# A hybrid encoder block: the inverse second stage of the long convolutions in three float32r part products, with tighter buffer rings

## The chip, the cores and the metric

The kernel is one program on one core of a Trainium2 chip. The metric is device time in microseconds (us) of one execution; a smaller number is better. Before the change it is 2696.65 us, the median of three runs.

Five engines work side by side, each with its own instruction queue that runs in order: PE (TensorE) multiplies matrices, DVE (VectorE), ACT (ScalarE) and POOL (GpSimd) do elementwise work, SP (SyncE) issues most of the transfers. PE writes its results into PSUM, a memory of eight banks; the other operands live in SBUF, 128 partitions wide.

## The reference, cut to what matters

The block mixes 2048 rows of 1024 channels. Half of the channels go through two long convolutions over the whole sequence; the rest (an mLSTM in both directions, projections, norms, an MLP) is not touched by the change.

```python
def two_sided_fft_conv(u, k_fwd, k_bwd, bias):
    S = u.shape[1]
    kern = jnp.concatenate([k_fwd, jnp.zeros_like(k_fwd[:1]), k_bwd[:0:-1]], axis=0)
    K = jnp.fft.rfft(kern, axis=0)
    U = jnp.fft.rfft(u, n=2 * S, axis=1)
    y = jnp.fft.irfft(U * K[None], n=2 * S, axis=1)[:, :S]
    return y + u * bias
...
z = cv[..., OFF_HV:OFF_HV + H_WIDTH]
z = cv[..., OFF_HX1:...] * two_sided_fft_conv(z, filt[:, 0, 0], filt[:, 1, 0], fb[0])
z = cv[..., OFF_HX2:...] * two_sided_fft_conv(z, filt[:, 0, 1], filt[:, 1, 1], fb[1])
```

The transform has length 4096 and 512 channels, all in float32. The two convolutions follow one another, since the second works on the gated result of the first.

## The kernel before, in words

**The convolutions.** The method `hyena` (from line 1053) does each transform of 4096 as two stages of matrix products, 64 by 64. The first stage of the data (`first`, line 1095) writes its result to a DRAM tensor `d1`; the spectra of the filters lie in `dk` already after their own first stage. The second stage is the loop of line 1175, once for each convolution (`o` is 0, then 1), over 32 frequency groups `j`. It is a software pipeline: in step `j` the code does

- `prepare(j + 1)`: the 128 by 128 matrix `c2` of the next group and its two operands `kd` (filter) and `rd` (data), each 128 by 512, are split into a high part rounded to float32r (a cast on ACT, line 166) and a low part, the remainder (a subtraction, line 169, here on POOL). The low parts of `kd` and `rd` are written over their sources, in the tiles `raw`;
- `spectrum(j)`: the product of `c2` and `kd` into a bank `pk`, as three part products (`mm3`, lines 159 to 161: low times high, high times low, high times high); `kept(j)` (line 1147) copies `pk` to SBUF on ACT;
- the inverse product of group `j - 2` (line 1187): matrix `ci` times the product spectrum `zz`, one plain float32 matmul into the bank `pi`, which ACT copies to `so` (line 1193), and every second step a store to `d2` is issued from ACT's queue;
- the product of `c2` and `rd` into `pu` (line 1191, three part products again);
- loads for later groups: `kernel_loads(j + 3)` (matrix `c2` into a tile `cr`, then `kd`), `data_loads(j + 3)` (`rd`), and `ci[j]` (line 1200), all issued from SP;
- `product(j)` (line 1154): five elementwise instructions on DVE that multiply the two spectra into `zz[j]`.

After each convolution's first half the loop of line 1228 (only for `o` = 0) does the inverse first stage with the gate and the first stage of the second convolution.

**What stands between.** PE does not wait for a step of the convolution: `long_conv` is a generator that yields a cost in us after each piece, and `drive` (line 217) fills that much of another generator, `work`, in between: the input projections (`convolved`, line 576, then `values_project`, line 679). In the first convolution a piece of `work` is 9, 9 or 6 matmuls of 128 by 512, with evictions on ACT (lines 607, 626), sums on DVE (line 613), and in two of four blocks a chunk of weights: a scaling on POOL (line 547), a cast on ACT (166), a subtraction on DVE (169). In the second convolution a piece is mostly 12 matmuls of 128 by 256. The order of all instructions on every engine is the order of the code (`manual_schedule`, line 294).

**Rings.** A tile is taken from a ring of `bufs` buffers in turn; the instruction that writes it waits for the last reader of what lay in it before. The rings here: `raw` 6, `hi` 4 (the high parts), `c` 4 (matrices in parts), `cr` 2, `ci` 3, `z` 4, `st` 2. [...]

Of the kernel before, what the change touches and what calls it, by code (L numbers as in the profile page):

```python
# [8 lines left out]
F32 = mybir.dt.float32  # L9
# [15 lines left out]
BIG = 1e30  # L25


SPLIT = {"w4", "s1k"}

# [13 lines left out]
def host_constants():  # L45
    f32 = np.float32
# [68 lines left out]
    out["c_s1"] = pack(s1, "s1")  # L115
    out["c_s1i"] = pack(s1i, "s1i")
    out["c_s1k"] = pack(s1k, "s1k")
    out["c_s2"] = np.ascontiguousarray(s2[:, data_row, :], dtype=f32)
    out["c_s2i"] = np.ascontiguousarray(s2i[:, :, back_col], dtype=f32)
    out["c_eye"] = np.eye(128, dtype=f32)  # L120
    out["c_rev"] = np.ascontiguousarray(np.eye(128, dtype=f32)[::-1])

# [25 lines left out]
class Builder:  # L148
# [904 lines left out]
    def hyena(self, pools):  # L1053
# [4 lines left out]
        d2 = [dt([32, 128, 512], f"d2{o}") for o in range(2)]  # L1058

        def raw(src):  # L1060
            t = wk.tile([128, 512], F32R, tag="raw", name="raw", bufs=6)
            self.load(t.bitcast(F32), src)
            return t

# [6 lines left out]

        def cols():
            return wk.tile([128, 256], F32R, tag="c", name="c", bufs=4)

        def constant(name):

# [13 lines left out]
            return wk.tile([128, 2, 512], F32, tag="st", name="st", bufs=2)  # L1090

        def short(dtype=F32):
            return wk.tile([128, 512], dtype, tag="z", name="z", bufs=4)

        def first(o, h, s1, x):

# [25 lines left out]
        for o in range(2):  # L1122
            kd, rd, c2, ci, kk, zz, pu = ({} for _ in range(7))

            def kernel_loads(j):
                c2[j] = wk.tile([128, 128], F32, tag="cr", name="cr", bufs=2)
                self.load(c2[j], io["c_s2"][j])
                kd[j] = raw(self.dk[j][:, o])

            def data_loads(j):  # L1130
                rd[j] = raw(d1[o][j])

            def prepare(j):
                c, src = cols(), c2[j]
                c2[j] = c[:, 0:128], c[:, 128:256]
                self.split(*c2[j], src, pool)
                kd[j], rd[j] = parts(kd[j]), parts(rd[j])

            def spectrum(j):
# [5 lines left out]
            def kept(j, pk):  # L1145
                kk[j] = short()
                act.copy(kk[j], pk)
                if j == 0:

                    kk["n"] = pair()[64:65, 0, :]  # L1150
                    act.copy(kk["n"], pk[64:65])
                    dve.memset(kk[j][64:65], 0.0)
# [14 lines left out]
            for j in range(2):  # L1167
                kernel_loads(j)
                data_loads(j)
            yield 14.0  # L1170
            prepare(0)
            kernel_loads(2)
            data_loads(2)
            yield 1.0
            for j in range(34):
                if j + 1 < 32:
                    prepare(j + 1)
                if j < 32:
                    pk = spectrum(j)
                    yield 1.3  # L1180
                    kept(j, pk)
                if j >= 2:
                    e = j % 2
                    if e == 0:
                        so = pair()
                    pi = self.pp.tile([128, 512], F32, tag="ptt", name="pi", bufs=1)
                    pe.matmul(pi, ci.pop(j - 2), zz.pop(j - 2), start=True, stop=True)
                    yield 1.3
                if j < 32:
                    pu[j] = bank("pu")  # L1190
                    self.mm3(pu[j], c2.pop(j), rd.pop(j), True, True)
                if j >= 2:
                    act.copy(so[:, e], pi)
                    if e == 1:
                        self.store(d2[o].rearrange("k (b j) c -> k b j c", b=4)[:, :, j - 3:j - 1, :], so)
                if j + 3 < 32:
                    kernel_loads(j + 3)
                    data_loads(j + 3)
                if j < 31 or j == 31:
                    ci[j] = wk.tile([128, 128], F32, tag="ci", name="ci", bufs=3)  # L1200
                    self.load(ci[j], io["c_s2i"][j])
                yield 1.3
                if j < 32:
                    product(j)
# [7 lines left out]

            def gate_loads(h):
                x[h] = [raw(d2[o][2 * h + r]) for r in range(2)]
                xg[h] = raw(self.tile_rows(1, h))

            def operand(h, r):
                if h < 16:
                    y.setdefault(h, []).append(parts(x[h][r], eng=(pool, dve)[r]))

            gate_loads(0)
            gate_loads(1)
            yield 12.0
            s1i, s1 = s1i(), s1()
# [3 lines left out]
            for h in range(17):  # L1228
                if h < 16:
                    py = bank("py")  # L1230
                    for r in range(2):
                        self.mm3(py, s1i[r], y[h][r], r == 0, r == 1)
                    y.pop(h)
                    yield 1.0
                    z = short()
                    dve.tensor_tensor(z, py, xg.pop(h).bitcast(F32), ALU.mult)
                operand(h + 1, 0)
                if h >= 1:
                    f = first(1, h - 1, s1, zt.pop(h - 1))
                    next(f)  # L1240
                    yield 1.0
                if h < 16:
                    zt[h] = parts(z, short(F32R), dve)
                operand(h + 1, 1)
                if h >= 1:
                    next(f)
                    yield 1.0
                    next(f, None)
                if h + 2 < 16:
                    gate_loads(h + 2)  # L1250


    def post(self, wk, src, wb, tmp, res, tag, eng):
# [727 lines left out]
```

## Time and profile before

| what | us |
|---|---|
| three runs, unprofiled: median (lowest, highest) | 2696.65 (2690.52, 2699.77) |
| the profiled execution: its own time | 2695.04 |
| its span, from the first to the last instruction | 2693.1 |
| second stage of the first convolution, in the span | about 482 to 679 |
| third stage and first stage of the second convolution | about 698 to 812 |
| second stage of the second convolution | about 812 to 1013 |

The profile is of one execution, of which the span lacks 1.94 us that lie around the instructions. The page gives busy time of each engine; the view of stretches gives the same by parts of the span, with the clock granted to PE as a share of full speed; the groups of instructions give count, busy time and mean duration of alike instructions and the idle time before them with what ended it. A line can be that of a helper: all three part products of all products stand under lines 159 to 161, so one goes by the names of tiles, written out<-in. Matmuls are pipelined: a recorded duration is longer than the distance from one start to the next, and that distance is what a matmul costs in a row of them.

### The profile page before, as it was taken

What the parts mean: (1) busy time and instruction counts of PE and PEld (TensorE: products, weight loads), DVE (VectorE), ACT (ScalarE), POOL (GpSimd) and SP (SyncE); (2) the same over time, 40 slices, a digit from 0 to 9 for tenths busy, and PEclk for the clock granted to TensorE, in tenths of its full rate; (3) what the DMA queues carried; (4) which work ended last, traced back from release to release, by engine and by line L of the source; (5) the groups of instructions that cost most, each with busy time, mean ns of one, the idle gap of its engine ahead of it and who ended that gap; (6) DMA issues with size and microseconds to landing.
All of it is one profiled execution on the core that took longest, in us unless ns stands there. A gap on an engine that the chain in (4) does not pass through costs nothing.

```text
span 2693.1 us, 35367 instructions
## 1 busy us (share of the span) xinstructions
PE 2590.1 (96%) x12237; PEld 2110.8 (78%) x12237; DVE 1544.1 (57%) x2454; ACT 1232.0 (46%) x2276; POOL 1204.1 (45%) x964
## 2 busy tenths in 40 slices
PE   6999999999999998889997999999999999999998
PEld 5778888777798887767774788868888888888876
DVE  5676653777547665666556444474444443543477
ACT  6355544655544346653334444454444323222344
POOL 1211114555225543446666877677772440301232
PEclk8999999999999999999998999999999999999999
DMA  6233346665676558556765444554447453445555
GB/s 175 61 87 113 114 125 219 194 190 176 217 233 178 185 167 275 180 166 218 241 200 186 156 137 164 184 191 172 146 155 287 147 176 100 130 141 163 181 170 213
DMA packets 288355, 465.74 MB, mean 173 GB/s; under 512 B 37543, under 2 KB 149415, under 8 KB 287153
## 3 DMA queue, kind: packets, MB, share of 16 engines
q1 hardware_dynamic: 227600, 324.85, 38.8%
q10 hardware_dynamic: 53264, 117.53, 11.6%
q0 software_dynamic: 7312, 21.11, 3.1%
q8 instruction: 97, 1.59, 0.2%
q14 instruction: 82, 0.66, 0.1%
HBM read 289.27 MB, written 174.13 MB: 172 GB/s over the span
## 4 chain that ended last, share of the span: by engine, by line
PE 40%; DVE 4%; POOL 4%; DMA 3%; issue 2%; ACT 2%; ACTq 0%; SPq 0%; DVEq 0%; POOLq 0%
PE pm L159 13%; PE pm L160 13%; PE pm L161 13%; DVE cb L169 1%; POOL xt L1265 1%; DMA m<-in_w_mlp_out_dram 1%; DMA hm<-ht 1%; DMA m<-in_w_mlp_in_dram 1%; POOL cb L169 1%; ACT xo L1405 1%; DVE hm L1906 0%; ACTq L234 0%; DVE xo L1408 0%; DVE gss L1307 0%; DVE hm L169 0%
## 5 line engine op out<-in xcount | busy, mean ns | idle before, releaser
L166 ACT CAST cb<-m 128x1024 fp32r<-128x1024 f32 (+1 forms) x342 | 277.9, 849 | 438.0 <-PE pm L159 375.3
L169 DVE TENSOR_TENSOR cb<-m,cb 128x1024 fp32r<-128x1024 f32 (+1 forms) x222 | 237.8, 1109 | 301.0 <-ACT cb L166 300.7
L160 PE MATMUL pm<-cb 128*128 128x512 f32 x880 | 343.6, 390 | 7.8 <-DVE cb L169 7.8
L159 PE MATMUL pm<-hm,cb 128*128 128x512 f32 x840 | 330.8, 394 | 13.9 <-POOL cb L169 8.0
L159 PE MATMUL pm<-cb 128*128 128x512 f32 x880 | 342.4, 389 | 1.2 <-DVE cb L169 1.0
L161 PE MATMUL pm<-cb 128*128 128x512 f32 x880 | 342.6, 389 | 0.0
L160 PE MATMUL pm<-hm,cb 128*128 128x512 f32 x840 | 329.9, 393 | 2.6 <-POOL hm L169 2.5
L161 PE MATMUL pm<-hm,cb 128*128 128x512 f32 x840 | 328.9, 392 | 0.0
L169 POOL TENSOR_TENSOR cb<-m,cb 128x1024 fp32r<-128x1024 f32 x120 | 262.0, 2194 | 61.7 <-ACT cb L166 61.6
L1717 DVE TENSOR_TENSOR m<-pm,m 128x512 f32<-128x512 f32 x224 | 153.9, 690 | 235.0 <-PE pm L161 214.3
L159 PE MATMUL pt<-hn,w 128*128 128x512 f32 x640 | 267.7, 419 | 1.0 <-ACT hn L489 0.9
L169 POOL TENSOR_TENSOR raw<-raw,hi 128x512 fp32r<-128x512 f32 x160 | 206.4, 1302 | 103.0 <-ACT hi L166 76.7
L160 PE MATMUL pt<-hn,w 128*128 128x512 f32 x640 | 252.0, 394 | 0.3 <-DVE hn L490 0.2
L161 PE MATMUL pt<-hn,w 128*128 128x512 f32 x640 | 251.9, 394 | 0.0
L160 PEld LDWEIGHTS pm<-cb 128*128 128x128 f32 x880 | 165.2, 188 | 45.7 <-DVE cb L169 11.7
L159 PEld LDWEIGHTS pm<-hm,cb 128*128 128x128 f32 x840 | 159.0, 189 | 50.0 <-POOL cb L169 10.2
L159 PEld LDWEIGHTS pm<-cb 128*128 128x128 f32 x880 | 165.2, 188 | 36.4 <-ACT junk L1891 1.4
L161 PEld LDWEIGHTS pm<-cb 128*128 128x128 f32 x880 | 165.3, 188 | 33.8
L160 PEld LDWEIGHTS pm<-hm,cb 128*128 128x128 f32 x840 | 159.4, 190 | 36.6 <-POOL hm L169 2.9
L1721 ACT ACTIVATE m<-m 128x512 f32<-128x512 f32 x128 | 80.6, 630 | 233.9 <-DVE m L1717 232.3
L161 PEld LDWEIGHTS pm<-hm,cb 128*128 128x128 f32 x840 | 159.4, 190 | 33.6
L647 POOL DMA_DIRECT2D vp<-vst x96 | 61.3, 643 | 228.1 <-ACT vst L643 227.0
(323 smaller groups left out, 5732.5 us busy)
## 6 DMA issues: line engine op xcount, KB each, us to landing
ga<-m ACTq DMA_DIRECT2D x96, 512.0 KB, 3.4
m<-ga SPq DMA_DIRECT2D x96, 512.0 KB, 4.1
d<-st ACTq DMA_DIRECT2D x64, 512.0 KB, 2.6
m<-in_w_mlp_in_dram SPq DMA_DIRECT2D x64, 512.0 KB, 4.0
m<-in_w_mlp_out_dram SPq DMA_DIRECT2D x114, 256.0 KB, 3.6
raw<-d SPq DMA_DIRECT2D x96, 256.0 KB, 3.0
xt<-in_x_dram SPq DMA_DIRECT2D x32, 512.0 KB, 5.5
dk<-kst SPq DMA_DIRECT2D x32, 512.0 KB, 3.3
```

Of the source, the lines that this page charges most:

```text
L159: pe.matmul(ps, w[1], x[0], start=first, stop=False)
L160: pe.matmul(ps, w[0], x[1], start=False, stop=False)
L161: pe.matmul(ps, w[0], x[0], start=False, stop=last)
L166: self.act.copy(hi, src)
L169: (eng_lo or self.dve).tensor_tensor(lo, src, hi.bitcast(F32), ALU.subtract)
L647: pool.dma_start(dst[:, 8 * b + e:8 * b + 8:2, cc:cc + 128], st[64 * e:64 * e + 64])
L1265: eng.tensor_tensor(res[:, cs], tmp[e], res[:, cs], ALU.add)
L1405: act.activation(x1, xt, AF.Square, accum_out=ss1[:, h:h + 1])
L1717: dve.tensor_tensor(dst, a, b, ALU.add)
L1721: act.activation(g, g, AF.Relu)
```

## The change

The names `s2` and `s2i` join the set of constants that the host rounds and delivers as high and low part side by side, 128 by 256 instead of 128 by 128. On the chip such a matrix is loaded into a tile `cr` of twice the size and passes one ACT copy into a tile `c` (`rounded`), which replaces the cast and the subtraction of `c2` and is new for `ci`. The inverse product takes `ci` in parts and `zz` in parts: `zz[j - 1]` is split in step `j` after `pu[j]`, high part to the ring `hi`, low part to the ring `z`. The ring `raw` goes from 6 to 5, `z` from 4 to 5, the ring `ci` is gone (`ci` and `c2` share `cr`), and loads and `prepare` take other places in the step. In the third stage the loads of the gate and of the next rows take other places too.

```diff
-SPLIT = {"w4", "s1k"}
+SPLIT = {"w4", "s1k", "s2", "s2i"}
...
-    out["c_s2"] = np.ascontiguousarray(s2[:, data_row, :], dtype=f32)
-    out["c_s2i"] = np.ascontiguousarray(s2i[:, :, back_col], dtype=f32)
+    out["c_s2"] = pack(s2[:, data_row, :], "s2")
+    out["c_s2i"] = pack(s2i[:, :, back_col], "s2i")
...
-            t = wk.tile([128, 512], F32R, tag="raw", name="raw", bufs=6)
+            t = wk.tile([128, 512], F32R, tag="raw", name="raw", bufs=5)
...
+        def matrix(src):
+
+            c = wk.tile([128, 256], F32, tag="cr", name="cr", bufs=2)
+            self.load(c, src)
+            return c
+
+        def rounded(src):
+            c = cols()
+            act.copy(c, src)
+            return c[:, 0:128], c[:, 128:256]
...
-            return wk.tile([128, 512], dtype, tag="z", name="z", bufs=4)
+            return wk.tile([128, 512], dtype, tag="z", name="z", bufs=5)
...
             def kernel_loads(j):
-                c2[j] = wk.tile([128, 128], F32, tag="cr", name="cr", bufs=2)
-                self.load(c2[j], io["c_s2"][j])
                 kd[j] = raw(self.dk[j][:, o])
...
             def prepare(j):
-                c, src = cols(), c2[j]
-                c2[j] = c[:, 0:128], c[:, 128:256]
-                self.split(*c2[j], src, pool)
+                c2[j] = rounded(c2[j])
                 kd[j], rd[j] = parts(kd[j]), parts(rd[j])
...
             for j in range(2):
                 kernel_loads(j)
                 data_loads(j)
+            c2[0] = matrix(io["c_s2"][0])
             yield 14.0
             prepare(0)
             kernel_loads(2)
-            data_loads(2)
+            c2[1] = matrix(io["c_s2"][1])
             yield 1.0
             for j in range(34):
-                if j + 1 < 32:
-                    prepare(j + 1)
                 if j < 32:
                     pk = spectrum(j)
                     yield 1.3
                     kept(j, pk)
+                    if j + 1 < 32:
+                        prepare(j + 1)
+                    if j + 2 < 32:
+                        data_loads(j + 2)
                 if j >= 2:
...
                     pi = self.pp.tile([128, 512], F32, tag="ptt", name="pi", bufs=1)
-                    pe.matmul(pi, ci.pop(j - 2), zz.pop(j - 2), start=True, stop=True)
+                    self.mm3(pi, ci.pop(j - 2), zz.pop(j - 2), True, True)
                     yield 1.3
                 if j < 32:
                     pu[j] = bank("pu")
...
+                if 1 <= j < 33:
+                    ci[j - 1] = rounded(ci[j - 1])
+                    zz[j - 1] = parts(zz[j - 1], short(F32R))
                 if j + 3 < 32:
                     kernel_loads(j + 3)
-                    data_loads(j + 3)
-                if j < 31 or j == 31:
-                    ci[j] = wk.tile([128, 128], F32, tag="ci", name="ci", bufs=3)
-                    self.load(ci[j], io["c_s2i"][j])
+                if j + 2 < 32:
+                    c2[j + 2] = matrix(io["c_s2"][j + 2])
+                if j < 32:
+                    ci[j] = matrix(io["c_s2i"][j])
                 yield 1.3
                 if j < 32:
                     product(j)
...
             def gate_loads(h):
                 x[h] = [raw(d2[o][2 * h + r]) for r in range(2)]
-                xg[h] = raw(self.tile_rows(1, h))
...
             gate_loads(0)
+            xg[0] = raw(self.tile_rows(1, 0))
             gate_loads(1)
...
                     dve.tensor_tensor(z, py, xg.pop(h).bitcast(F32), ALU.mult)
+                    if h + 1 < 16:
+                        xg[h + 1] = raw(self.tile_rows(1, h + 1))
+                    if h + 2 < 16:
+                        gate_loads(h + 2)
...
-                if h + 2 < 16:
-                    gate_loads(h + 2)
```

## The prediction, made before the changed kernel was run

> **What bounds the kernel now.** I read the page first, then the view of stretches for the stages that the change touches, then the order of PE's instructions in one of them.
>
> ```profile
> span 2693.1 us, 35367 instructions
> ...
> PE 2590.1 (96%) x12237; PEld 2110.8 (78%) x12237; DVE 1544.1 (57%) x2454; ACT 1232.0 (46%) x2276; POOL 1204.1 (45%) x964
> ```
>
> ```profile
> 480.00:676.00 196.00, 196.00 (x801) 150.12 (x800) 154.14 (x250) 111.76 (x214) 109.24 (x108) 1.00 0.62 189
> 676.00:812.00 136.00, 133.46 (x778) 117.32 (x777) 66.67 (x133) 62.26 (x115) 37.66 (x32) 0.99 0.68 222
> 812.00:1014.00 202.00, 199.00 (x1307) 173.79 (x1306) 136.58 (x234) 94.00 (x186) 100.55 (x104) 0.99 0.58 175
> 879.00:885.00 6.00, 4.99 (x24) 4.52 (x25) 3.21 (x8) 3.02 (x6) 3.02 (x3) 0.72 0.50 172
> ```
>
> A row has the stretch, its length, then the busy us (and count) of PE, PEld, DVE, ACT and POOL, the granted clock, and the DMA share. The first row of stretches is the second stage of the first convolution ("round one"), the third row that of the second ("round two"). In round one PE is busy for 196.00 of 196.00 us; in round two for 199.00 of 202.00. ACT is busy for 111.76 us of round one (57%), POOL for 109.24 (56%). So in both rounds the path that sets the end is PE's own queue: what PE no longer does is gained, and each us that PE must wait is lost. Busy alone does not prove it, since recorded matmuls overlap; the distances of starts do.
>
> ```profile
> 600.38 0.39 PE L161 MATMUL pu<-hi,c 128*128 128x512 f32 x1
> ...
> 606.74 0.39 PE L161 MATMUL pk<-hi,c 128*128 128x512 f32 x1
> ...
> 609.03 1.02 PE L1187 MATMUL pi<-z,ci 128*128 128x512 f32 x2
> ...
> 610.13 0.40 PE L160 MATMUL pt<-hn,w 128*128 128x512 f32 x1
> 610.36 0.39 PE L161 MATMUL pt<-hn,w 128*128 128x512 f32 x1
> ...
> 614.72 1.02 PE L1187 MATMUL pi<-z,ci 128*128 128x512 f32 x2
> ```
>
> A row of PE starts one 128x512 float32r matmul every 0.23 us (610.13 to 610.36), with no hole. The plain product starts at 609.03 and the second matmul behind it at 610.13: 1.10 us for it and one float32r matmul, so it costs 0.87.
>
> ```profile
> L1187 PE MATMUL pi<-z,ci x128: 590/591/668, 491.3 to 1012.8; 128*128 128x512 f32 x128
> L1193 ACT COPY st<-pi x64: 574/586/594, 492.4 to 1013.5; 128x512 f32<-128x512 f32 x64
> ```
>
> There are two records to a plain product, so 64 products; 64 copies of the result say the same.
>
> **The change part by part.** *PE.* Three part products cost 3 x 0.23 = 0.69 us in place of 0.87: 0.18 less, 64 times, **-11.5 us**. The same matmuls of the same shape run in `pk` and `pu`, so this term is sure to a few tenths. The Trainium skill ("FP8 and Floating Point Precision", section TensorE Precision Notes) says that true FP32 takes four passes through the array; by that rule one pass of four goes, an estimate of 0.23 us each and 14.7 us in all, with which the sum below would be 3.2 us lower. The measured distance decides: 0.87 is less than four passes of 0.23.
>
> *ACT and POOL.* What is added has rows of its own kind.
>
> ```profile
> L169 POOL TENSOR_TENSOR raw<-raw,hi 128x512 fp32r<-128x512 f32 x64 | 82.3, 1302 | 6.3 <-ACT hi L166 3.2 <-PE pk L161 1.6
> ...
> L166 ACT CAST hi<-raw 128x512 fp32r<-128x512 f32 x63 | 37.3, 620 | 12.4 <-PE pu L161 7.2 <-POOL c L169 3.2 <-POOL raw L169 2.0
> ...
> L1147 ACT COPY z<-pk 128x512 f32<-128x512 f32 x32 | 18.6, 582 | 23.2 <-PE pk L161 21.6 <-issue 1.5
> ...
> L169 POOL TENSOR_TENSOR c<-cr,c 128x128 fp32r<-128x128 f32 x32 | 15.8, 493 | 75.9 <-ACT c L166 75.9
> ...
> L547 POOL TENSOR_TENSOR wf<-wf,eps 128x512 f32<-128x512 f32 x12 | 12.5, 1045 | 0.0
> ...
> L166 ACT CAST c<-cr 128x128 fp32r<-128x128 f32 x31 | 9.1, 294 | 2.0 <-ACT st L1193 2.0
> ...
> L166 ACT CAST w<-wf 128x512 fp32r<-128x512 f32 x11 | 6.8, 620 | 12.0 <-POOL wf L547 11.2 <-ACT st L1193 0.8
> ```
>
> ACT: per step a cast of a 128x128 matrix (0.29 us) goes; two copies of 128x256 come, which no row shows here; between 0.29 for 128 columns and 0.62 for 512 they cost about 0.40 each. The high part of `zz` is one more cast of 0.62. Together +1.13 us a step. POOL: the subtraction of the matrix goes (0.49), that of `zz` comes (1.30): +0.81. Over 32 steps ACT goes from 112 to 148 us of round one's 196, POOL from 109 to 135. Neither becomes the bound by its sum; what counts is the order, since both queues run in order and more of each now stands between two products of PE.
>
> *The starts.* `prepare(1)` used to stand ahead of `spectrum(0)`; now it stands behind `kept(0)`.
>
> ```profile
> 482.83 0.39 PE L161 MATMUL pk<-hi,c 128*128 128x512 f32 x1
> ...
> 483.27 0.59 ACT L1147 COPY z<-pk 128x512 f32<-128x512 f32 x1 [1.52 <-PE pk L161]
> ...
> 483.88 0.58 ACT L1151 COPY st<-pk 1x512 f32<-1x512 f32 x1
> ...
> 485.14 0.39 PE L159 MATMUL pk<-hi,c 128*128 128x512 f32 x1
> ```
>
> The last matmul of the first `pk` starts at 482.83, ACT copies from 483.27 and 483.88 (to 484.46), and PE starts the next `pk` at 485.14. In the new order ACT still owes the matrix (0.40) and `kd` (0.62), to 485.5, and POOL the low part (1.30), to 486.9 with its handover. The second of the three matmuls reads that low part, so `pk` may start at 486.7: about 1.5 us late, in each round: **+3.0** (2 to 4; nothing hides it, as the piece of projection work in between is already counted in 485.14).
>
> *The ends.* `zz[30]` is split only after the last `pu`, `zz[31]` after its product, and the inverse products follow at once.
>
> ```profile
> 1008.16 0.39 PE L161 MATMUL pu<-hi,c 128*128 128x512 f32 x1
> ...
> 1009.83 1.02 PE L1187 MATMUL pi<-z,ci 128*128 128x512 f32 x2
> ...
> 1011.56 0.69 DVE L1165 TENSOR_TENSOR z<-z,pu 128x512 f32<-128x512 f32 x1
> ...
> 1012.35 1.10 PE L1187 MATMUL pi<-z,ci 128*128 128x512 f32 x2
> ```
>
> For `zz[30]`: last `pu` matmul 1008.16, cast from 1008.6 to 1009.2, low part to 1010.6, so its `pi` can start at 1010.4 instead of 1009.65 (1009.83 less one saving): 0.7. For `zz[31]`: DVE ends at 1012.25, cast and subtraction to 1014.3, start at 1014.1 instead of 1012.35, of which 0.7 is already counted: 1.5 more. Round one's end is built alike: twice 2.2, **+4.4** (2 to 5).
>
> *In the steps.* In a plain step the chain fits just in time: the same 0.44 + 0.62 + 1.30 from the last `pu` matmul to the low part of `zz` against a `pk` and at least one piece of projection (2 us) on PE. It does not fit where a chunk of projection weights falls between `pi` and `pu`.
>
> ```profile
> 607.04 2.53 POOL L169 TENSOR_TENSOR raw<-raw,hi 128x512 fp32r<-128x512 f32 x2
> ...
> 609.53 1.04 POOL L547 TENSOR_TENSOR wf<-wf,eps 128x512 f32<-128x512 f32 x1
> ...
> 610.61 0.62 ACT L166 CAST w<-wf 128x512 fp32r<-128x512 f32 x1 [2.23 <-POOL wf L547]
> ...
> 611.13 0.58 ACT L1193 COPY st<-pi 128x512 f32<-128x512 f32 x1
> ```
>
> Before the change POOL works off two subtractions (2.53), then the scaling of the weights (1.04); ACT waits 2.23 us for that, and the copy of `pi` stands behind it on ACT at 611.13. This cost nothing, as nothing urgent stood there. In the new order `prepare` starts behind the `pk` of 606.74: copy 607.2 to 607.8, matrix to 608.2, `kd` to 608.8, POOL's two subtractions to 611.4, scaling to 612.4, cast of the weights to 613.1, copy of `pi` to 613.7, `ci` to 614.1, `zz` high to 614.7, low to 616.1. The `pi` that PE starts at 614.72 (614.54 after the saving) can start at 615.8: 1.3 us late. Round one has 12 chunks (the row of line 547); a step has three places for a piece of work, so a third of them, four, fall here: 5.2. In the other two places the wait comes ahead of `kept`, where `kd` has more room; I take 0 to 1 each, 0.4 on the mean: 3.2. Together **+8.4** (2 to 15).
>
> *Loads.* SP issues as many DMAs as before; matrices bring 64 KB more each. But `c2[j + 2]` is now issued behind `kd[j + 3]`, whose `raw` buffer (ring 5) is free only after `pu[j]`, and ACT needs it one step later, with `kd`, `rd`, the copy of `pi`, `ci` and `zz` queued behind.
>
> ```profile
> cr<-in_c_s_dram SPq DMA_DIRECT2D x64, 64.0 KB, 4.5
> ci<-in_c_s2i_dram SPq DMA_DIRECT2D x64, 64.0 KB, 2.6
> ```
>
> From the last `pu` matmul (600.38) to the `pi` two steps on that reads the `zz` behind this chain (609.03) PE has 8.65 us, 8.47 after the saving. The chain: 0.44 to the release, 0.37 for the issue of `kd`, the landing, then ACT 0.40 + 0.62 + 0.62 + 0.58 + 0.40 + 0.62 = 3.24, POOL 1.38, less 0.23: 5.2 plus the landing. It fits while the matrix lands within 3.3 us. The row `ci` (2.6; the issue order puts it behind a 256 KB load, as `c2` will be) says it fits, the row `cr` (4.5) that it does not; I take the first with a few stragglers: **+1** (0 to 9). The ring `z` (5) and `c`, `hi` (4, now with three and two tiles a step) wait only on readers that are already counted. The third stage's loads go ahead by part of a pass or, for the gate, back by one; the most they can gain is PE's idle there (136.00 - 133.46 = 2.5), and I take 0.
>
> *A price on long waits.* What a wait of PE costs beside itself:
>
> ```profile
> 879.67 0.39 PE L159 MATMUL pt<-w,hn 128*128 128x256 f32 x1 [2.10 <-ACT w L166]
> ...
> 881.45 0.63 PE L160 MATMUL pu<-raw,c 128*128 128x512 f32 x1
> 881.87 0.63 PE L161 MATMUL pu<-hi,c 128*128 128x512 f32 x1
> ```
>
> After a wait of 2.10 us (and a shorter one behind it) the next 512-column matmuls start 0.42 apart, and the stretch from 879 to 885 has a granted clock of 0.72: 0.28 x 6 = 1.7 us more. My waits of 1 to 1.5 us lie below that. The Trainium skill ("TensorE: Matmul & The Clock Gate", section Why this matters for your kernels) advises no PE-idle gaps beyond about 3 us; by that rule no wait of this size costs extra and the sum stands; the trace shows that 2.1 us can be enough, which only the slower rival below uses.
>
> **Sum.** -11.5 + 3.0 + 4.4 + 8.4 + 1 = +5.3 us on the profiled execution's 2695.04 (span 2693.1 and 1.94 around it): 2700.3. The median of the runs is 1.6 above that execution, so the time is **2702**. A measurement of this kernel can tell about 0.3%, 8.1 us, from no change: the band of "same" is 2688.6 to 2704.7, and the forecast is no change that can be told, on its slower half; its own range is 2693 to 2705.
>
> **Rivals.** *A, the waits stay covered: faster.* ACT is idle for 84 of round one's 196 us, and if its queue runs ahead of PE as it did, the chunks hide. For it: the wait of 2.23 us moved nothing before. Against it: the starts and ends are plain chains with nothing to cover them. If of these only about 2 us remain: 2696.65 - 11.5 + 2 = **2687**.
>
> *B, the matrix lands late: slower.* One mechanism: ACT stands in front of `c2` in every step. It decides from a landing of 3.3 us on. At 4.5 us a step is short by 1.2 us; about half of round one's 32 steps have the short distance computed above, and as a wait lengthens the next distance, half of the amount shows: 16 x 1.2 = 19, half 9.5. Round two has longer distances (202 us for 32 steps against 196) and adds none. In place of the 1 in the sum: 2702 + 8.5, and where it meets a chunk a wait passes 2.1 us and brings the clock's 1.7, twice: **2714**. For it: the row `cr`, and 128 KB more per step. Against it: `ci`.
>
> *C, the plain product is not what counts:* PE could be held by something else behind it. The distances without a hole speak against it; it would give 2696.65 plus the waits, beyond B, and I give it no chance of its own.
>
> **How the numbers follow.** Forecast (same) 0.42, A (faster) 0.20, B and larger waits at chunks (slower) 0.38. The range leaves out a tenth on each side: from A's middle, 2687, to just past B's, 2716.
>
> **What the profile after would show.** Under `pi` three matmuls at 0.23 in place of the two records. Right: PE idle of 10 to 20 us in the two second stages, with `pi` waiting for POOL's subtraction of `zz` and, at each round's start, the second `pk` for that of `raw`; ACT's casts of weights still waiting for line 547. A would show PE without idle in round one; B would show ACT's copy of the matrix waiting for the DMA of `cr` in most steps and a granted clock below 1.00 in round one. The prediction is wrong if PE's idle there stays under 3 us or passes 25, or if the third stage moves by more than 3 us.

## The result, and the profile after

The changed kernel takes **2723.8 us** (median of four runs, 2720.1 to 2727.14) against 2698.21 us for the kernel before in the same comparison (four runs, 2690.52 to 2699.93). The ratio is 1.0107, with a 95% interval of 1.0094 to 1.0121: 25.6 us slower by the medians, where no change was forecast, in a range of 2693 to 2705, and the wider range ended at 2716.

The page of the changed kernel, its span and its engines:

```profile
span 2724.0 us, 35381 instructions
...
PE 2597.4 (95%) x12301; PEld 2126.3 (78%) x12301; DVE 1550.1 (57%) x2454; ACT 1286.7 (47%) x2404; POOL 1256.9 (46%) x964
```

PE has 64 matmuls more, ACT 128 casts more, and POOL as many instructions as before, of which 64 have become longer. The span is 30.9 us longer; of that, 5.2 us is the draw of the two profiled executions (the one before lay 3.2 us under its median, the one after 2.0 over).

The view of stretches, with the same columns as before (length, busy time of PE, PEld, DVE, ACT, POOL, granted clock, DMA share, and last the GB/s moved):

```profile
480.00:676.00 196.00, 185.10 (x775) 144.90 (x774) 142.49 (x232) 128.77 (x259) 122.55 (x99) 0.99 0.62 194
676.00:812.00 136.00, 131.80 (x702) 111.80 (x701) 73.02 (x138) 67.20 (x123) 42.84 (x36) 0.99 0.65 220
812.00:1014.00 202.00, 191.56 (x1292) 174.24 (x1290) 135.18 (x228) 112.09 (x231) 117.69 (x93) 0.97 0.62 192
```

PE is no longer full. In round one it now has 10.9 us without a record, and in the same 196 us it gets through 775 matmuls instead of 801 (by records, of which a product of `pi` has three now and had two before). ACT and POOL are still far from full: 66% and 63% of the stretch. So no engine became the bound by its sum; something makes PE wait.

The instructions of the tile `pi`, and what PE waited for ahead of them:

```profile
L160 PE MATMUL pi<-z,c x64: 387/395/628, 495.2 to 1042.1; 128*128 128x512 f32 x64
...
its engine sat idle before it (us, times) until:
  POOL z L169: 29.0, 37
  ACT hi L166: 9.1, 11
```

The plain products are gone. The last two rows count weight loads and matmuls apart, so a product can stand in them twice; by products, 25 of 64 wait for POOL's low part of `zz` and 7 for ACT's high part. Those are the last links; what made them late stands one queue further back. The view of waits shows it, for the stretch from 482 to 700 (round one) and from 812 to 1046 (round two); a row has the time waited, how often, and the longest:

```profile
ACT w L166 <- POOL wf L547: 32.0, 12, 3.1
ACT c L1083 <- DMA cr<-in_c_s_dram: 16.1, 11, 2.6
PEld pi L160 <- POOL z L169: 12.2, 15, 1.2
...
ACT c L1083 <- DMA cr<-in_c_s_dram: 31.9, 23, 5.7
PEld pi L160 <- POOL z L169: 7.3, 10, 1.9
```

In round one ACT stands 32.0 us before the scaled weights (18.7 in the same stretch before the change, 11.2 of them up to 676), and in both rounds it stands before the matrix `c2` that has not landed, in round two for 31.9 us in 23 steps. What PE needs next is queued behind these two waits; how much of them reaches PE is another matter.

To see where that reaches PE, I took the start of each matmul after, less the start of the same matmul before. The table gives this shift in us at places named by the time in the kernel before. A shift that grows is a wait, one that falls is work saved; the level at 482 comes from what ran ahead of the stage.

| kernel | 482 | 660 | 700 | 812 | 830 | 860 | 876 | 900 | 1005 | 1013 |
|---|---|---|---|---|---|---|---|---|---|---|
| changed | 1.8 | 15.4 | 17.2 | 17.8 | 20.8 | 20.4 | 29.9 | 24.6 | 28.0 | 29.9 |

Round one (482 to 700) loses 15.4 us net, the third stage (700 to 812) 0.6, round two (812 to 1013) 12.1.

### The profile page after: what moved, and what is told of

It is laid out like the page before. It is cut to its first block, busy times and chain, and to the rows that moved or that the text cites. A ratio compares the mean times of both kernels' runs of the same rounds, so it can differ in the third digit from the quotient of the medians.

```text
span 2724.0 us, 35381 instructions
## 1 busy us (share of the span) xinstructions
PE 2597.4 (95%) x12301; PEld 2126.3 (78%) x12301; DVE 1550.1 (57%) x2454; ACT 1286.7 (47%) x2404; POOL 1256.9 (46%) x964
## 3 DMA queue, kind: packets, MB, share of 16 engines
q10 hardware_dynamic: 53264, 117.53, 11.5%
## 4 chain that ended last, share of the span: by engine, by line
PE 38%; DVE 4%; POOL 4%; DMA 3%; issue 3%; ACT 2%; ACTq 0%; SPq 0%; DVEq 0%; POOLq 0%
PE pm L159 13%; PE pm L161 13%; PE pm L160 13%; DVE cb L169 1%; POOL cb L169 1%; POOL xt L1280 1%; DMA m<-in_w_mlp_out_dram 1%; DMA m<-in_w_mlp_in_dram 1%; ACT xo L1420 1%; DVE hm L1921 0%; DVE hm L1851 0%; DVE hm L169 0%; DVE m L1732 0%; DVE xo L1423 0%; DVE gss L1322 0%
## 5 line engine op out<-in xcount | busy, mean ns | idle before, releaser
L159 PE MATMUL pt<-hn,w 128*128 128x512 f32 x640 | 258.5, 404 | 1.2 <-ACT hn L489 1.1
L160 PE MATMUL pt<-hn,w 128*128 128x512 f32 x640 | 252.5, 395 | 0.5 <-DVE hn L490 0.4
L161 PE MATMUL pt<-hn,w 128*128 128x512 f32 x640 | 252.8, 395 | 0.0
L159 PEld LDWEIGHTS pm<-hm,cb 128*128 128x128 f32 x840 | 159.2, 189 | 51.3 <-POOL cb L169 10.8
```

The lines of the kernel that those rows point to most:

```text
L159: pe.matmul(ps, w[1], x[0], start=first, stop=False)
L160: pe.matmul(ps, w[0], x[1], start=False, stop=False)
L161: pe.matmul(ps, w[0], x[0], start=False, stop=last)
```

## The experiments

Each kernel below was timed against the kernel before on the same chip, and I give its ratio as a loss in us of 2696; the changed kernel's, so counted, is 28.8 (25 to 33). Where a text speaks of theories M and W: **M** says that the matrix `c2` is requested too late, **W** that the weight chunk's scaling holds up ACT.

**The products alone.** In the kernel before, only the plain product becomes three float32r ones. They read one constant matrix, and `zz` is rounded by DVE; the true matrix and the low part of `zz` are left out:

```diff
-                z = zz[j] = short()
+                z = short()
...
-                dve.tensor_tensor(z, z, p, ALU.add)
+                zz[j] = short(F32R)
+                dve.tensor_tensor(zz[j], z, p, ALU.add)
...
-                    pe.matmul(pi, ci.pop(j - 2), zz.pop(j - 2), start=True, stop=True)
+                    zr = zz.pop(j - 2)
+                    self.mm3(pi, (wx[0][:, 0:128], wx[0][:, 128:256]), (zr, zr), True, True)
```

> The kernel before, with the inverse product as three float32r matmuls and nothing else of the change. The matrix is one constant in two parts and zz is written by its last DVE instruction as float32r, so nothing is split; the true matrix and the low part of zz are left out, the loads stay. If PE's term was sized rightly (64 x 0.18), the time is 11 to 12 us below the kernel before. If the plain product is not what PE waits for there, less than 3 us below.

Measured: 2686.57 us (2683.76 to 2688.06), ratio 0.996 (0.9945 to 0.9974): 10.8 us faster. Its shift falls from 0.6 at 482 to -5.3 at 700, so round one saves 5.9 us; 32 products at 0.18 make 5.8. In round two each product saves its 0.17 to 0.18 too, but the shift falls by 3.0 only: between 860 and 900, where six products should lower it by 1.0, it rises by 0.7. The first term of the sum holds, and 39.6 us were lost elsewhere (10.8 + 28.8).

**The matrix one piece earlier (M).**

```diff
                         prepare(j + 1)
                     if j + 2 < 32:
+                        c2[j + 2] = matrix(io["c_s2"][j + 2])
                         data_loads(j + 2)
...
-                if j + 2 < 32:
-                    c2[j + 2] = matrix(io["c_s2"][j + 2])
```

> The changed kernel, with the load of c2[j + 2] issued right behind prepare(j + 1) instead of at the end of the step behind the load of kd. Theory M (the matrix lands late and ACT stands before it): round two's waits go, and the kernel is 10 to 14 us below the changed kernel, that is 11 to 16 us above the one before. Theory W (the weight chunks hold ACT and POOL): at most 3 us below the changed kernel, 22 to 26 us above the one before.

Measured: 2716.06 us (2712.75 to 2718.54), ratio 1.0072 (1.0053 to 1.009): 19.4 us slower, so 9.4 of the 28.8 are gone. In its waits (rows of round one, then of round two) the matrix has nearly left, and the weights are as late as ever:

```profile
ACT w L166 <- POOL wf L547: 32.0, 12, 3.1
ACT c L1083 <- DMA cr<-in_c_s_dram: 1.5, 2, 1.2
...
ACT c L1083 <- DMA cr<-in_c_s_dram: 6.9, 3, 4.0
```

M holds a part of the loss, not the whole.

**POOL relieved.** The low part of `zz` is subtracted on DVE instead of POOL, so that POOL has two splits a step as in the kernel before:

```diff
-                    zz[j - 1] = parts(zz[j - 1], short(F32R))
+                    zz[j - 1] = parts(zz[j - 1], short(F32R), dve)
```

> The changed kernel, with the low part of zz subtracted on DVE instead of POOL. Theory W, in the form that POOL's queue is the trouble: POOL has 1.3 us less in every step, the inverse product waits less, and 6 to 10 us of the 25.6 us loss go. Theory M: less than 3 us go, since ACT still stands before the matrix.

Measured: 2721.39 us (2718.54 to 2727.7), ratio 1.0093 (1.0074 to 1.0112): 25 us slower, so 3.8 are gone where this form of W asked for 6 to 10. In round one ACT waits 19.0 us for scaled weights instead of 32.0, but a new wait has come:

```profile
ACT w L166 <- POOL wf L547: 19.0, 9, 3.1
...
ACT hi L166 <- DVE z L1172: 11.3, 13, 1.8
```

The split on DVE delays the product behind it, and ACT's next cast of `zz` waits for that. POOL's share of work is not the point by itself.

**The scaling one piece earlier (W).** The scaling of a weight chunk is put one piece of projection ahead of its cast on ACT:

```diff
             if live and b == 1:
                 ahead(i // 4 + 1, 0)
+            if live and b > 1:
+                ahead(i // 4 + 1, b - 1, True)
```

> The changed kernel, with the scaling of each weight chunk (line 547) put into POOL's queue one piece of projection work ahead of its cast on ACT. Theory W: ACT's 32.0 us of waiting for line 547 in round one shrink by more than half and 8 to 12 us of the 25.6 us loss go. Theory M: less than 2 us go.

Measured: 2715.49 us (2713.47 to 2721.68), ratio 1.0072 (1.0054 to 1.009): 19.4 us slower, again 9.4 gone. In round one:

```profile
ACT c L1088 <- DMA cr<-in_c_s_dram: 26.4, 20, 2.6
...
ACT w L166 <- POOL wf L547: 6.1, 6, 1.9
```

The wait for the weights falls from 32.0 to 6.1 us, and that for the matrix rises from 16.1 to 26.4: part of the time that ACT gained it spent before the next late thing. So I tried both together, with a control.

**Both moves.**

> The changed kernel with both moves together: the second-stage matrix is requested one piece earlier, right behind the preparing of the step before, and a weight chunk is scaled on GpSimd one piece ahead of its ScalarE cast. Each move alone took about 9 us off a loss of 25 to 28. Theory M+W (two separate waits, the landing of the matrix and the scaling of the chunk): the gains add, 28 - 9 - 9 = 10 us slower than the kernel before, 8 to 12. Rival O (each move alone only lets the other wait appear in the same place, as the matrix wait of ScalarE that rose from 16 to 26 us in round one when the scaling was moved): together they give more than the sum, 0 to 6 us slower. Rival P (GpSimd's third split of each step holds what is left, whatever ScalarE waits for): at most 14 us gone, 12 to 19 us slower, and TensorE's waits for GpSimd's low parts stay near the 12 and 7 us of the changed kernel.

Measured: 2703.55 us (2700.52 to 2706.28), ratio 1.0029 (1.0017 to 1.0041): 7.8 us slower. 21 of 28.8 us are gone, where the two alone make 18.8: separate waits that add. The 2.2 us beyond the sum are within the intervals.

**Control:** the scaling one piece earlier in the kernel before.

> Control: the kernel before, with only the scaling of a chunk one piece ahead of its cast. The kernel before waits 11 us on ScalarE for scaled chunks in round one, but its TensorE is covered there. Theory W (the wait counts only because the changed step has no room left): no change, within 3 us. Rival: the wait costs the kernel before as well, then 4 to 9 us faster, and the gain of this move in the changed kernel says nothing of the change.

Measured: 2698.98 us (2693.8 to 2702.55), ratio 1.0012 (1.0002 to 1.0021): 3.2 us slower, barely outside of no change, and not faster. In its trace the shift is 6.4 us at 482, before the stage begins, and 6.6 at 1013: through both rounds the move did nothing, though from 482 to 700 ACT's wait for the weights falls from 18.7 to 4.3 us. ACT's 11.2 us before the scaled weights cost the kernel before nothing, as the prediction had said; the same wait costs in the changed kernel.

The move has a price of its own, ahead of the stage. In the kernel with both moves:

```profile
401.52 1.04 POOL L547 TENSOR_TENSOR wf<-wf,eps 128x512 f32<-128x512 f32 x1 [5.40 <-DMA wf<-in_w_in_dram]
...
403.30 0.50 PE L159 MATMUL p<-hi,c 128*128 128x512 f32 x1 [1.39 <-POOL c L169]
```

One chunk lands late, and its scaling now stands in POOL's queue before the low part of a matrix that PE needs next. At the two matmuls of 401.6 and 401.9 in the kernel before, the shift grows by 2.4 to 3.4 us in each of the six kernels with the scaling early, the control among them, and in none of the others. So the 7.8 us of both moves hold 2.6 that arise there and not in the rounds.

The shifts of these kernels, read as above:

| kernel | 482 | 660 | 700 | 812 | 830 | 860 | 876 | 900 | 1005 | 1013 |
|---|---|---|---|---|---|---|---|---|---|---|
| products alone | 0.6 | -4.6 | -5.3 | -5.3 | -5.2 | -6.3 | -6.1 | -5.6 | -8.4 | -8.3 |
| matrix early | 1.5 | 9.5 | 11.0 | 11.0 | 14.0 | 13.5 | 22.7 | 19.2 | 18.3 | 20.2 |
| scaling early | 4.2 | 9.6 | 11.0 | 9.9 | 12.8 | 12.4 | 22.8 | 17.6 | 19.0 | 20.9 |
| both | 2.7 | -0.1 | 1.4 | 0.4 | 3.4 | 2.9 | 11.1 | 7.6 | 6.7 | 9.1 |
| no split of `zz` | 2.1 | 2.8 | 2.1 | 1.7 | 4.2 | 4.1 | 15.9 | 10.8 | 9.6 | 9.7 |

Round one's loss of 15.4 becomes 9.5 with the matrix early, 6.8 with the scaling early, and a gain of 1.3 with both. Round two's loss of 12.1 only falls to 9.2, 11.0 and 8.7. So round one is explained. In round two the matrix early mends one stretch: from 900 to 1005 the changed kernel loses 3.4, and with the matrix early that is a gain of 0.9. What is left there sits mostly in one place, 860 to 900, where the kernel with both moves loses 4.7 net. ACT's order of work there in that kernel:

```profile
858.00 0.35 ACTq L234 DMA_DIRECT2D de_d<-cw  x1
...
866.61 0.41 ACT L1088 CAST c<-cr 128x256 fp32r<-128x256 f32 x1 [3.99 <-DMA cr<-in_c_s_dram]
...
869.89 0.62 ACT L166 CAST hi<-raw 128x512 fp32r<-128x512 f32 x1 [2.35 <-DMA raw<-d]
...
872.79 0.41 ACT L1088 CAST c<-cr 128x256 fp32r<-128x256 f32 x1 [1.78 <-DMA cr<-in_c_s2i_dram]
873.10 0.61 ACT L166 CAST hi<-z 128x512 fp32r<-128x512 f32 x1
```

Three loads in a row land late, and PE's `pi` waits 2.42 us for the last cast. SP had issued them at 859.32, 859.75 and 861.64, so they took 7 to 11 us. The transfers of that stretch, from 857 to 873 in 40 slices:

```profile
DMA  4000100099903109736555465111969999999999
GB/s 146 3 0 0 1 0 0 0 87 143 5 0 8 3 15 56 28 13 10 13 18 10 46 36 20 20 36 20 292 266 430 410 433 402 392 348 374 370 383 407
```

Each slice is 0.4 us. But for two slices, almost nothing moves for about 11 us, and then up to 430 GB/s. ACT of the kernel before stands at the same place in the work too:

```profile
866.48 0.62 ACT L166 CAST hi<-raw 128x512 fp32r<-128x512 f32 x1 [3.78 <-DMA raw<-d]
```

There the loads have more distance, and what PE loses behind it are the 2.10 us at 879.67 that the prediction quoted.

What makes the hole was not tried, but the traces hold a trail. In all twelve, ACT issues the store `de_d<-cw` there (858.00 above): 0.5 KB, 128 packets of 4 bytes, for the work in between. The first packet that takes more than 3 us starts 2.1 to 2.7 us after that issue, and between 100 and 2650 us no other packet of up to 2 KB takes so long in any trace. A like store 25 us earlier (`st_d`, packets of 8 bytes) is followed by some 4 us with little traffic, and by no packet of more than 3 us. In the trace above traffic is low already at 857.4, so it is the long packets that follow the store. No run moves it, and its part in the hole is not shown.

**All three moves.** Both moves and the low part on DVE:

> The changed kernel with the matrix early, the scaling early and the low part of the spectrum product on VectorE, so that GpSimd has two splits a step as in the kernel before. M+W: the third move adds nothing beyond its 3 to 4 us, 5 to 9 us slower than the kernel before. P: with GpSimd as free as before, the gain of the products shows, between 5 us faster and 4 slower. Rival D (VectorE in order: the split waits behind the product and ScalarE's next high part behind the split, 11 us of such waits in the run with VectorE alone): no better than both moves without it, 8 to 14 us slower.

Measured: 2708.3 us (2707.41 to 2715.3), ratio 1.0056 (1.0037 to 1.0074): 15.1 us slower, worse than without DVE and just beyond the 8 to 14 of rival D. Round two loses 14.3 (shift 4.0 at 812, 18.3 at 1013). The mechanism of that rival, DVE in order, is in the trace: in round one of this kernel ACT waits for the product, and DVE for ACT.

```profile
ACT hi L166 <- DVE z L1177: 17.1, 19, 1.8
DVE z L169 <- ACT hi L166: 13.8, 19, 1.0
```

**Starts and ends.** With both moves, both first matrices requested at the outset, `prepare(1)` ahead of the first product again, and the last two low parts of `zz` of each round on DVE:

```diff
             prepare(0)
             kernel_loads(2)
             yield 1.0
+            prepare(1)
...
-                    zz[j - 1] = parts(zz[j - 1], short(F32R))
+                    zz[j - 1] = parts(zz[j - 1], short(F32R), pool if j < 31 else dve)
```

> The changed kernel with the matrix early, the scaling early, the second step of each round prepared ahead of the first product, and the last two products of each round split on VectorE instead of GpSimd. Against the run with the two moves alone: the starts give back 3 us (1.6 and 1.5 measured) and the ends 1 to 3 of their 4, so 4 to 6 us less than that run. Rival: the starts only move the wait to the first product, which then comes later by the second step's two splits, 2 us each; then no difference from that run within 2 us.

Measured: 2704.03 us (2699.07 to 2708.59), ratio 1.0033 (1.0021 to 1.0046): 8.9 us slower, no gain over both moves alone. In its trace the start of round one does cost nothing (shift 5.6 at 482 and at 500, against 2.7 and 4.1), but the end of round one costs more (1.3 at 660, 5.0 at 700: 3.7 against 1.5). I expected 4 to 6 us; the start's 1.4 came, and DVE gave it back: at round one's end ACT's cast of `zz[31]` waits 1.81 us for DVE's product.

**Data as far ahead as before.** Both moves, `raw` 6 again with `data_loads(j + 3)` at the end of the step, paid for by the ring `z`:

```diff
-            t = wk.tile([128, 512], F32R, tag="raw", name="raw", bufs=5)
+            t = wk.tile([128, 512], F32R, tag="raw", name="raw", bufs=6)
...
-            return wk.tile([128, 512], dtype, tag="z", name="z", bufs=5)
+            return wk.tile([128, 512], dtype, tag="z", name="z", bufs=3)
...
-                    zz[j - 1] = parts(zz[j - 1], short(F32R))
+                    zz[j - 1] = parts(zz[j - 1], wk.tile([128, 512], F32R, tag="zl", name="zl", bufs=1))
                 if j + 3 < 32:
                     kernel_loads(j + 3)
+                    data_loads(j + 3)
```

> The run with both moves (matrix early, scaling early: 8 us slower than the kernel before), and the data loads as far ahead as in the kernel before: ring raw 6 again, data of group j + 3 requested at the end of step j; paid for by a ring z of 3 and one buffer of its own for the low part of the product spectrum. What is left of the loss lies in round two, where at 862 to 873 us ScalarE waits 4.0, 2.35 and 1.78 us for a matrix, for data and for a matrix that land 7 to 11 us after their issue, and TensorE stands behind it. Theory D (the shorter distance of the data loads holds part of that): 2 to 5 us less than that run, 3 to 6 us slower than the kernel before, ScalarE's wait for data gone. Rival: all three land late together, and with the data early the two matrices still end the wait: no change within 2 us, 6 to 10 us slower than before.

Measured: 2707.86 us (2705.56 to 2709.98), ratio 1.0048 (1.0035 to 1.006): 12.9 us slower. The rival holds for the place itself: round two loses 9.2 (shift 2.6 at 812, 11.8 at 1013), as without it. ACT no longer waits for the data there, but 3.35 us for the one matrix and 4.38 for the other. The further 5 us by the medians arise outside of the two rounds, ahead of 482 (shift 5.1 there, against 2.7) and behind 1013, and I cannot say from what.

**No split.** The changed kernel without the split of `zz`:

```diff
-                z = zz[j] = short()
+                z, zr = short(), short(F32R)
+                zz[j] = zr, zr
...
-                dve.tensor_tensor(z, z, p, ALU.add)
+                dve.tensor_tensor(zr, z, p, ALU.add)
...
-                    zz[j - 1] = parts(zz[j - 1], short(F32R))
```

> The changed kernel without the split of the product spectrum: the last operation of the product writes it as float32r, all three part products take that tile as both parts, and its high-part cast on ScalarE and subtraction on GpSimd, 32 of each a round, are left out, so the low part of the product spectrum is missing from what is computed. Loads, rings, the place of the preparing and the rounding copies stay as in the changed kernel. If the split holds the loss (its 0.62 us on ScalarE and 1.3 on GpSimd a step, and the ends of the rounds), the gain of the products shows: 5 to 10 us faster than the kernel before. If the late matrix, the moved preparing and the weight chunks hold it whatever the split does: 8 to 20 us slower than the kernel before.

Measured: 2703.49 us (2700.11 to 2705.95), ratio 1.0027 (1.0017 to 1.0037): 7.3 us slower, just under what the second theory asked for and far from the first. Its waits in round one:

```profile
ACT w L166 <- POOL wf L547: 27.5, 12, 4.3
...
ACT c L1083 <- DMA cr<-in_c_s_dram: 20.0, 17, 3.1
...
PEld pk L160 <- POOL raw L169: 5.8, 8, 1.2
```

Both waits of ACT are still there, yet round one loses nothing net (2.1 at 482 and at 700). So neither the waits nor the split is the cause alone. A step's chain on ACT and POOL is too long for PE's distance when the split, the late matrix and the late weights come together: without the split, or without the two waits, round one is even or better. Round two loses 8.0, most of it again in the hole of the transfers.

No version that computes everything beats the kernel before. The products are worth 10.8 us; the kernel with both moves still pays 1.4 and 3.0 in the first 18 us of the two rounds, 1.5 and 2.4 in their last, and 4.7 in the hole: 13.0 net, against 6.6 that it gains in all the rest between 482 and 1013.

## Why the prediction was wrong

**PE: right.** -11.5 predicted, -10.8 measured with the products alone. By round one's shift the distance of starts decides: 5.9 saved, 5.8 by 0.18 a product. The four passes of the Trainium skill ("FP8 and Floating Point Precision", section TensorE Precision Notes) would make 7.4 of it by the estimate (half of 14.7), which that shift does not show; the interval of the ratio (7.0 to 14.8) holds both.

**Starts: right.** PE's rows of round one's second `pk`, in the changed kernel:

```profile
487.30 0.51 PE L159 MATMUL pk<-hi,c 128*128 128x512 f32 x1 [0.16 <-ACT hi L166]
488.71 0.50 PE L160 MATMUL pk<-raw,c 128*128 128x512 f32 x1 [0.90 <-POOL raw L169]
```

The first matmul would have started at 486.99 (485.14 and the 1.85 that all is late) and starts at 487.30; the second follows after 1.41 instead of 0.23, 1.2 more. That is 1.5 us as predicted, with POOL's `raw` named; ahead of 830 in round two the shift grows by 3.0, of which the second `pk` has 1.5.

**Ends: right in size, partly wrong in how.** Predicted 4.4, measured 2.15 in round one and 2.0 in round two. The parts differ: in round one `zz[30]` costs 1.4 and `zz[31]` 0.8, for 0.7 and 1.5. And the step "`zz[30]` is split only after the last `pu`" failed in round two:

```profile
1035.56 0.62 ACT L166 CAST hi<-z 128x512 fp32r<-128x512 f32 x1
...
1040.13 0.62 ACT L166 CAST hi<-z 128x512 fp32r<-128x512 f32 x1 [0.73 <-DVE z L1172]
```

The last matmul of the last `pu` starts at 1035.95, after the cast of `zz[30]` has begun: this cast waits for ACT's queue and not for `pu`. `zz[30]` cost nothing there, and `zz[31]` all of the 2.0.

**In the steps: right mechanism, half the size.** This is the first step that failed: "four, fall here: 5.2 ... Together +8.4 (2 to 15)". Round one's waits come to 21.2 us (15.4 net and the 5.8 saved); less start and end, 17.5 fall in its steps, where 8.4 + 1 were predicted. Five chunks of weights fall ahead of a `pi`, and at these products PE waits 1.5, 2.4, 2.9, 2.0 and 1.6 us: 10.4 in place of 5.2. The fourth is the very chunk that the prediction works through, with 2.0 for 1.3. Its first rows in the changed kernel:

```profile
618.10 0.39 PE L161 MATMUL pk<-hi,c 128*128 128x512 f32 x1
618.61 0.77 ACT L607 ACTIVATE yc<-pt,cw 128x512 f32<-128x512 f32 x1
619.26 0.58 ACT L1154 COPY z<-pk 128x512 f32<-128x512 f32 x1
```

From the copy of `pk` on, the chain takes the 8.9 us that were written (607.2 to 616.1; here 619.26 to 628.18). But the copy starts 1.16 us behind the last matmul of `pk`, not 0.46, since ACT is still at an eviction of the projections: that is the missing 0.7. The third of the five, on POOL, ACT and PE:

```profile
574.43 2.55 POOL L169 TENSOR_TENSOR raw<-raw,hi 128x512 fp32r<-128x512 f32 x2 [1.04 <-PE pi L161]
576.93 1.04 POOL L547 TENSOR_TENSOR wf<-wf,eps 128x512 f32<-128x512 f32 x1
...
578.01 0.62 ACT L166 CAST w<-wf 128x512 fp32r<-128x512 f32 x1 [3.14 <-POOL wf L547]
578.54 0.58 ACT L1203 COPY st<-pi 128x512 f32<-128x512 f32 x1
579.02 0.40 ACT L1083 CAST c<-cr 128x256 fp32r<-128x256 f32 x1
579.32 0.62 ACT L166 CAST hi<-z 128x512 fp32r<-128x512 f32 x1
...
579.99 0.49 PE L159 MATMUL pi<-hi,c 128*128 128x512 f32 x1 [0.75 <-ACT hi L166]
581.41 0.50 PE L160 MATMUL pi<-z,c 128*128 128x512 f32 x1 [0.92 <-POOL z L169]
```

This is the chain as written: two subtractions, scaling, weights, copy, `ci`, `zz`. PE waits twice in one product, 0.75 and 0.92, and here it pays a price that I had put at nothing: "My waits of 1 to 1.5 us lie below that". From 581.80 the granted clock is 0.50 for 3.4 us, which is 1.7 us more; in round one this happens once. The other 7 us, this price among them, lie elsewhere in the steps, where 3.2 and the loads' 1 stood. With both moves 16.7 us of the loss are gone: it was the matrix and the weights.

**Loads: wrong.** This is the step that decided: "I take the first with a few stragglers: +1", and "Round two has longer distances ... and adds none". The rows of the issues in the changed kernel:

```profile
cr<-in_c_s_dram SPq DMA_DIRECT2D x64, 128.0 KB, 3.6
cr<-in_c_s2i_dram SPq DMA_DIRECT2D x64, 128.0 KB, 3.2
```

My own limit was a landing of 3.3 us; the median is 3.6. I had derived the limit and then took the row that lay on the safe side of it. And round two, where I had put nothing, is where ACT waits longest for the matrix, 31.9 us against 16.1. Most of that wait stays on ACT: with the matrix early, 2.9 us of round two's net loss go (12.1 to 9.2). The mean distance (202 us for 32 steps) said nothing of the place where transfers stall for 11 us, although the kernel before shows that place too, by ACT's wait of 3.78 us for `raw<-d`. Round two's waits come to 17.9 us (12.1 and 5.8), 14.4 of them neither start nor end; I had counted none. Of these, the late matrix is shown for the stretch behind 900; for 860 to 900, what holds up the transfers stays open.

**The rivals.** B, the late matrix, was the nearest. It had the mechanism and the limit, and placed it in round one only; its 2714 replaced the 1 us of loads without enlarging the chunks, and in the chip's sum both came. The third stage moved by 0.6 us, and recorded idle in the two stretches is 21.3 us (10.9 and 10.4), inside the bounds of 3 and 25 that I had set for being wrong: a bound on recorded idle was a poor test. A matmul is recorded as 0.39 long where its distance in a row is 0.23, and as 0.50 behind a wait (the rows at 487 to 489), so part of each wait is recorded as busy, and so is what a lower clock costs.

## What to carry to other kernels

When PE is full and a change puts more work into in-order queues beside it, write down the longest chain from one product to the next, every queue entry included, and compare its slack with each wait that the other engines already have: a wait of 11 us that costs nothing today is priced once the slack is gone, and several such waits add. Take a derived limit at its word when the rows lie around it, and look for the worst stretch of the transfers and not the median or the mean distance. Before writing such a change, try its gain alone, as with the products here: these 10.8 us (7 to 15 by the interval) are about the most that an arrangement of the rest can leave.

## What the runs showed of the hardware

The granted clock can halve after waits that are short, and what counts is how much of them falls into one stretch of 3.4 us. In the traces the granted clock changes only at times that lie whole multiples of 3.41 us apart. On that grid, in the changed kernel (length, PE's busy time, and the clock as the last column but two):

```profile
544.20:547.60 3.40, 2.00 (x8) 1.09 (x6) 3.28 (x6) 2.40 (x5) 2.34 (x3) 1.00 0.90 307
578.40:581.80 3.40, 1.73 (x7) 0.91 (x6) 3.05 (x5) 3.40 (x9) 1.27 (x1) 1.00 0.64 213
581.80:585.20 3.40, 3.40 (x10) 2.64 (x9) 2.77 (x6) 2.57 (x5) 2.88 (x3) 0.50 0.53 188
...
885.60:889.00 3.40, 1.51 (x8) 1.02 (x8) 2.28 (x4) 2.91 (x7) 2.25 (x2) 1.00 1.01 352
889.00:892.40 3.40, 3.40 (x16) 3.19 (x15) 0.62 (x2) 2.36 (x6) 3.40 (x4) 0.50 0.75 227
```

The stretch at 578 holds PE's waits of 0.75 and 0.92 us, the one at 885 two of 1.04 and 0.85:

```profile
886.73 0.50 PE L159 MATMUL pk<-hi,c 128*128 128x512 f32 x1 [1.04 <-ACT hi L166]
888.08 0.50 PE L160 MATMUL pk<-raw,c 128*128 128x512 f32 x1 [0.85 <-POOL raw L169]
```

PE is without a record for 1.67 and 1.89 us of them, and 3.4 us at a clock of 0.50 follow. The stretch at 544 touches a pair just as long (0.95 and 0.92), but only 1.40 us of idle fall into it, and the clock stays. Over the twelve traces, between 482 and 1050 us, every such stretch at the full clock with 1.9 us or more of idle is followed by the lower clock and none with 1.4 or less; in between both occur. The Trainium skill ("TensorE: Matmul & The Clock Gate", section Why this matters for your kernels) advises against gaps beyond about 3 us; the trace shows that two waits of about 1 us can be enough, and the measurement decides.

And transfers can stall for some 11 us in a program that keeps moving around them: the hole of 857 to 868 above, at 0 to 56 GB/s in most slices, while the share of busy DMA engines is between 0 and nine tenths. In every trace its long packets follow the store `de_d<-cw`; whether that store makes the hole was not tried.
